# An encoder layer on one core: split first loads, squares and evictions, row tiles fetched three steps ahead, and a second output buffer for four compact tiles

## The chip, the core and the metric

The kernel is one program on one core of a Trainium2 chip. The metric is the device time of one execution in microseconds (us). The profile names the engines PE (TensorE, matmuls), PEld (its weight loads), DVE (VectorE), ACT (ScalarE), POOL (GpSimd) and SP (SyncE, which here only issues transfers). A matmul's result lies in one of the banks of the accumulator memory; a bank can be used again only after ACT and DVE have read it out, which is called evicting here.

## The reference

One layer of a bidirectional encoder is applied to two batches with the same weights: a prompt of 1024 rows and a sample of 512 rows, each row 1024 wide.

```python
h = rms_norm(x, pre_w)
cols = h @ w_in           # q|k, v, o, gates, z of branch A; q, k, v, z of branch B; merge gates
y_a = o * headnorm(mlstm_fwd + mlstm_bwd) * silu(z_a)       # 4 heads x 256, chunks of 128
y_b = mix(three dilated window attentions, 8 heads x 64) * silu(z_b)
merged = sigmoid(g_a) * (y_a @ w_proj_m) + sigmoid(g_b) * (y_b @ w_proj_a)
out = x + rms_norm(merged @ w_out, post_w)
```

All is in float32. The three attention groups have the windows and dilations (128, 1), (512, 4) and (2048, 16).

## The kernel before

**Products.** A float32 product is made of three matmuls on split operands: each operand is a high part (ACT's rounded copy) and a low part (DVE's difference), and `mm3` (L233 to L235) issues high x high, low x high, high x low. So every operand of a product, a weight or a row tile, passes ACT and DVE first: weights at L296 (ACT, `wh`) and L302 (DVE, `wl`).

**The beginning.** The first value columns are computed by a scheme of block combinations: `value_group` issues products of combined blocks named B11, B21 and so on. `lead` prepares B11: for each of the four row tiles of 128 rows it takes the sum of squares (`root`: ACT squares at L320, POOL makes the mean and the power -1/2 at L321 and L322), scales the identity by the result (L406, `u2b`), and PE turns and scales the row tile with it (L408) into four banks, k = 0 to 3, each 128 x 512. Then each bank is evicted as a high part (ACT, L412) and a low part (DVE, L413). PE's first value product (L233 to L235, tiles `d<-v,Hh`) reads them. Behind it stand the squares of the other four row tiles (ACT, L422), their scaling (DVE, L427), and the pieces of B21: for k = 0 to 3 `put` turns four row tiles on PE (L446), evicts the bank (ACT, L453), adds a matmul that takes the high part away (L459) and copies the low part (ACT, L460). `with_m1` sets where those pieces stand between the matmuls.

**The second half.** From 1720 us on, attention tiles of the branch B stand between the matmuls of the output branches. `branches` builds the work of one block of 512 rows: before a unit of projection, the rows of branch A's output, tiles of 128 x 512, are fetched from memory into three buffers in turn (`rows_in`: sraw, ymr0, ymr1) and split into high and low parts by `split`, ACT at L2121, DVE at L2122. `along` advances this generator once in three or four steps of the unit that runs. The fetches are issued on POOL's queue (L274), as are the weights w_out and w_pm (L285). An engine runs its instructions in the order in which they were written, so a wait at the head of its queue delays all behind it. `final` is the output product: two banks named `dense` are filled in turn, and each is evicted by ACT (L2231, the squares) and DVE (L2233, the product with the post weight) before PE may use it again.

**Compact attention tiles.** For the group with the largest dilation, `compact` computes four tiles at a time and gathers their output in a buffer `ot`: DVE copies the sums (L1707, `ot<-st`), ACT the output (L1708), and two stores (SP, L249) bring it to `og_b`. For the sample there is one such buffer for four tiles (`four`), so that L1707 of the next four must wait for both stores. `sg`, a tile of 512 columns, is used by the gates elsewhere.

Of the kernel before, what the change touches and what calls it, by code (L numbers as in the profile page):

```python
# [22 lines left out]
F32 = mybir.dt.float32  # L23
F32R = mybir.dt.float32r
AF = mybir.ActivationFunctionType
OP = mybir.AluOpType
# [3 lines left out]
P = 128  # L30
D = 1024
KT = D // P
BLK = 512
# [4 lines left out]
EPS = 1e-6  # L38
# [5 lines left out]
OW = 132  # L44
# [160 lines left out]
class Net:  # L205
# [111 lines left out]
    def root(self, xt, r, junk):  # L317
# [5 lines left out]
        return r[:, 2:3]  # L323

    def norm(self, xt, r, junk, pw=None):
# [64 lines left out]
    def combos(self, ps, H, xt, r, junk, pw, plus, minus, again, diag):  # L390
# [12 lines left out]
        def lead():  # L403
            ps_ = [ps.tile([P, BLK], F32, name="d") for _ in range(4)]
            for t in range(4):
                nc.vector.tensor_scalar(diag[t], self.ident, self.root(xt[0][t], r[t], junk), None, op0=OP.mult)  # L406
                for k in range(4):
                    nc.tensor.matmul(ps_[k][:, t * P:(t + 1) * P], a0[t][:, k * P:(k + 1) * P], diag[t], start=t == 0,  # L408
                                     stop=True, skip_group_check=True)
            for k in range(4):  # L410
                hi, lo, w = H[0][B11][:, k], H[1][B11][:, k], self.prew[:, k:k + 1]
                self.high = nc.scalar.activation(hi, ps_[k], AF.Copy, scale=w)  # L412
                self.low = nc.vector.scalar_tensor_tensor(lo, ps_[k], w, hi.bitcast(F32), op0=OP.mult, op1=OP.subtract)  # L413

        roots = {}

        def norm(i, t, j):

            if i and j and t % 2 == 0:
                two = r[4 + t // 2].rearrange("p (a b) -> p a b", a=3)  # L420
                for a in range(2):
                    nc.scalar.activation(junk, xt[i][t + a], AF.Square, accum_out=two[:, 0, a:a + 1])  # L422
                nc.gpsimd.tensor_scalar(two[:, 1], two[:, 0], 1.0 / D, EPS, op0=OP.mult, op1=OP.add)
                nc.gpsimd.tensor_tensor(two[:, 2], two[:, 1], self.mhalf, op=OP.pow)
                roots.update({t: two[:, 2, :1], t + 1: two[:, 2, 1:]})
            x, c = xt[i][t], slice(j * BLK, (j + 1) * BLK)
            return nc.vector.scalar_tensor_tensor(x[:, c], x[:, c], roots[t] if i else r[t][:, 2:3], pw[:, c], op0=OP.mult, op1=OP.mult)  # L427
# [165 lines left out]
    def value_group(self, T, H, us, co, ps, begin, wide):  # L593
# [27 lines left out]
        if True:  # L621
# [3 lines left out]
            def with_m1():  # L625
# [8 lines left out]
                low.append(split(wa[:, 1]))  # L634
                with self.tc.issue_after(last.ins), self.tc.issue_after(self.splits[1].ins):
# [7 lines left out]
                low.append(last.ins)  # L643
                rest = [put(B21, 0)]
                yield
                for k in range(1, 4):
                    rest.append(put(B21, k))
                    rest.pop(0)()
                rest.pop(0)()
                yield  # L650
# [1226 lines left out]
    def attend(self, T, fill, steps, first, banks, outs, after=None, beside=None, at=()):  # L1877
# [5 lines left out]
        with ExitStack() as st:  # L1883
# [18 lines left out]
            else:  # L1902
                o = sb.tile([P, outs * OW], F32, name="ot", bufs=1)
                self.ot = Rot(self, [o[:, i * OW:(i + 1) * OW] for i in range(outs)])
                four = Rot(self, [o[:, :4 * OW]])

# [191 lines left out]

    def split(self, T, b, row, places, halves):

# [9 lines left out]
        for j, (hi, lo) in enumerate(halves):  # L2110
            for k in range(6):
                if k < 4:
                    r = row + 4 * j + k
                    t = self.rows_in.pop(0)
                    self.rows_in.append(t)
                    got.append(t)
                    with self.tc.issue_after(self.loaded.ins):
                        self.fetch(("ym", T.S, min(r // 2, 4)), t[:, :w], T.ym[r, :, b * BLK:b * BLK + w], self.side)
                if k > 1:
                    t = got.pop(0)  # L2120
                    nc.scalar.activation(hi[:, k - 2, :w], t[:, :w], AF.Copy)  # L2121
                    nc.vector.tensor_sub(lo[:, k - 2, :w], t[:, :w], hi[:, k - 2, :w].bitcast(F32))  # L2122
                yield
# [20 lines left out]
    def branches(self, T, b, odd, before):  # L2144
# [28 lines left out]
        def proj_a(weights):  # L2173
            for ct in range(KT):
# [5 lines left out]
                for k in range(4):  # L2180
# [4 lines left out]
                    if k == 3:  # L2185
# [6 lines left out]

        return (self.along(before, lambda: self.split(T, b, 0, [(odd, 0, 1), (odd, 2, 1)], yb), 3)
                + self.along([Unit([(a["w_pm"][ct],) for ct in range(KT)], proj_m)],
                             lambda: self.split(T, b, 8, [(1 - odd, 1, 2)], ya), 4)
                + [Unit([(a["w_pa"][ct],) for ct in range(KT // 2)], proj_a)])
# [84 lines left out]
def body(tc, a):  # L2281
# [3 lines left out]
    with ExitStack() as st:  # L2285
# [12 lines left out]
        with ExitStack() as s1:  # L2298
# [4 lines left out]
            with ExitStack() as sv:  # L2303
# [21 lines left out]
                nc.scalar.dma_start(N.prew, a["prewc"])  # L2325
                for t in range(4):
                    rows(0, t)
                weights(0, 0)
                for t in range(4):
# [107 lines left out]
        with ExitStack() as s1:  # L2437
# [35 lines left out]
            with ExitStack() as s2:  # L2473
# [3 lines left out]
                nc.gpsimd.memset(N.sraw, 0.0)  # L2477
                N.sg = Rot(N, [sp.tile([P, BLK], F32R, name="sg")])
                ym = N.pool(s2, "ym", 1, "right")
# [105 lines left out]
```

## Time and profile before

| what | value |
|---|---|
| three runs | 2191.48, 2193.38, 2189.7 us; median 2191.48 |
| the profiled execution | 2191.66 us |
| its span in the trace | 2189.9 us |
| mean granted clock of PE | 1.0 |
| busy share | PE 99%, PEld 85%, DVE 67%, ACT 50%, POOL 32% |
| waits of PE that the list shows | 3.2 us before its first matmul, for a load; eight others, from 0.2 to 1.0 us, 3.8 us in all |

A row of the timeline gives start and duration in us, engine, line, operation, output and inputs; in brackets the idle time of the engine just before it and what ended that. Matmuls overlap: the start of one to the start of the next is the pace. In a row of a group, the last numbers are the busy time in us, the mean of one in ns, and the idle time before.

### The profile page before, as it was taken

What the parts mean: (1) busy time and instruction counts of PE and PEld (TensorE: products, weight loads), DVE (VectorE), ACT (ScalarE), POOL (GpSimd) and SP (SyncE); (2) the same over time, 40 slices, a digit from 0 to 9 for tenths busy, and PEclk for the clock granted to TensorE, in tenths of its full rate; (3) what the DMA queues carried; (4) which work ended last, traced back from release to release, by engine and by line L of the source; (5) the groups of instructions that cost most, each with busy time, mean ns of one, the idle gap of its engine ahead of it and who ended that gap; (6) DMA issues with size and microseconds to landing.
All of it is one profiled execution on the core that took longest, in us unless ns stands there. A gap on an engine that the chain in (4) does not pass through costs nothing.

```text
span 2189.9 us, 33604 instructions
## 1 busy us (share of the span) xinstructions
PE 2175.2 (99%) x11626; PEld 1857.3 (85%) x11626; DVE 1457.3 (67%) x2923; ACT 1085.2 (50%) x2227; POOL 702.2 (32%) x990
## 2 busy tenths in 40 slices
PE   9999999999999999999999999999999999999998
PEld 8988888888888888888888889998788888888887
DVE  7766564657778555547888765574668755656674
ACT  7322333344444333446777666666755544544332
POOL 1000332333333222326677650011045522232331
PEclk9999999999999999999999999999999999999999
DMA  3641454733333222367646558877768786776773
GB/s 138 190 141 67 151 162 144 229 108 116 112 110 116 78 77 97 135 227 250 218 158 219 183 172 255 236 237 202 200 234 275 242 295 198 227 244 200 239 241 106
DMA packets 205460, 395.62 MB, mean 181 GB/s; under 512 B 36361, under 2 KB 117961, under 8 KB 205290
## 3 DMA queue, kind: packets, MB, share of 16 engines
q1 hardware_dynamic: 174984, 281.39, 40.5%
q0 software_dynamic: 26704, 99.50, 14.2%
q10 hardware_dynamic: 3602, 12.59, 1.4%
q8 instruction: 92, 1.51, 0.3%
q14 instruction: 78, 0.64, 0.1%
HBM read 274.71 MB, written 118.69 MB: 180 GB/s over the span
## 4 chain that ended last, share of the span: by engine, by line
PE 92%; issue 1%; DMA 1%; DVE 1%; POOL 0%; ACT 0%; DVEq 0%; POOLq 0%
PE d L234 13%; PE d L233 13%; PE d L235 13%; PE dense L233 13%; PE dense L235 12%; PE dense L234 12%; PE lg L1771 2%; PE pt L1801 1%; PE o L1844 1%; PE num L233 1%; PE num L235 1%; PE num L234 1%; DMA sraw<-ym_a 1%; PE num L1467 1%; PE o L1823 1%
## 5 line engine op out<-in xcount | busy, mean ns | idle before, releaser
L233 PE MATMUL dense<-H,wh 128*128 128x512 f32 x664 | 269.5, 406 | 0.0
L234 PE MATMUL dense<-H,wh 128*128 128x512 f32 x664 | 260.4, 392 | 0.0
L235 PE MATMUL dense<-H,wl 128*128 128x512 f32 x664 | 260.4, 392 | 0.0
L233 PE MATMUL d<-Hh,phla 128*128 128x512 f32 x608 | 236.5, 389 | 0.0
L235 PE MATMUL d<-Hh,phla 128*128 128x512 f32 x608 | 236.5, 389 | 0.0
L234 PE MATMUL d<-Hl,phla 128*128 128x512 f32 x608 | 236.5, 389 | 0.0
L302 DVE TENSOR_TENSOR wl<-wraw,wh 128x1024 fp32r<-128x1024 f32 (+1 forms) x121 | 150.4, 1245 | 50.0 <-ACT wh L296 49.9
L235 PE MATMUL d<-Hh,phlb 128*128 128x512 f32 x456 | 177.4, 389 | 0.0
L233 PE MATMUL d<-Hh,phlb 128*128 128x512 f32 x456 | 177.4, 389 | 0.0
L234 PE MATMUL d<-Hl,phlb 128*128 128x512 f32 x456 | 177.4, 389 | 0.0
L296 ACT ACTIVATE wh<-wraw 128x1024 fp32r<-128x1024 f32 (+1 forms) x124 | 128.1, 1036 | 67.0 <-PE dense L234 20.7
L235 PEld LDWEIGHTS dense<-H,wl 128*128 128x128 f32 x664 | 124.7, 188 | 28.1
L764 POOL TENSOR_TENSOR psum_w<-pw_raw 128x512 f32<-128x512 f32 x38 | 55.4, 1458 | 276.7 <-DMA pw_raw<-w_in 206.9
L233 PEld LDWEIGHTS dense<-H,wh 128*128 128x128 f32 x664 | 125.1, 188 | 16.8 <-issue 1.2
L234 PEld LDWEIGHTS dense<-H,wh 128*128 128x128 f32 x664 | 125.3, 189 | 14.7
L1790 DVE CUSTOM_DVE_ANT_0 ls<-lg,bias 128x256 f32<-128x256 f32 (+2 forms) x240 | 78.8, 350 | 86.6 <-PE lg L1771 61.5
L234 PEld LDWEIGHTS d<-Hl,phla 128*128 128x128 f32 x608 | 114.1, 188 | 23.7
L233 PEld LDWEIGHTS d<-Hh,phla 128*128 128x128 f32 x608 | 114.1, 188 | 23.7
L235 PEld LDWEIGHTS d<-Hh,phla 128*128 128x128 f32 x608 | 114.1, 188 | 23.7
L782 POOL TENSOR_TENSOR psum_w<-pw_raw,psum_w 128x512 f32<-128x512 f32 x38 | 49.3, 1298 | 251.7 <-DVE phla L746 251.7
L1794 ACT ACTIVATE ls<-ls,nm 128x256 f32<-128x256 f32 (+1 forms) x192 | 87.3, 456 | 73.0 <-DVE nm L1792 48.0
L233 PE MATMUL d<-v,Hh 128*128 128x484 f32 (+1 forms) x336 | 121.3, 361 | 0.2
(657 smaller groups left out, 5834.5 us busy)
## 6 DMA issues: line engine op xcount, KB each, us to landing
pw_raw<-w_in SPq DMA_DIRECT2D x76, 512.0 KB, 4.1
wraw<-w_in SPq DMA_DIRECT2D x63, 512.0 KB, 4.4
aqk_a<-pwk SPq DMA_DIRECT2D x32, 512.0 KB, 6.9
wraw<-w_pm POOLq DMA_DIRECT2D x24, 512.0 KB, 6.0
wraw<-w_out POOLq DMA_DIRECT2D x24, 512.0 KB, 4.1
Q<-aqk_a SPq DMA_DIRECT2D x20, 512.0 KB, 6.2
wraw<-w_v POOLq DMA_DIRECT2D x22, 430.0 KB, 6.5
aqk_b<-sw SPq DMA_DIRECT2D x36, 256.0 KB, 6.7
```

Of the source, the lines that this page charges most:

```text
L233: nc.tensor.matmul(out, lh, rh, start=start, stop=False, **kw)
L234: nc.tensor.matmul(out, lh, rl, start=False, stop=False, **kw)
L235: nc.tensor.matmul(out, ll, rh, start=False, stop=stop, **kw)
L296: high = nc.scalar.activation(hi[:, :n], raw[:, :n], AF.Copy)
L302: low = (self.lows or nc.vector).tensor_sub(lo[:, :n], raw[:, :n], hi[:, :n].bitcast(F32))
L764: self.nc.gpsimd.tensor_add(s[:, 0], ws[1][:, 0], ws[1][:, 1])
L782: nc.gpsimd.tensor_sub(s[:, 1], wa[:, 1], s[:, 1])
L1467: nc.tensor.matmul(pn, hi[:, j], z[:, c1], start=j == 0 and z is v[0], stop=False)
L1771: nc.tensor.matmul(lg[:, hh], q[hh][:, qs], z.rearrange("p (n j) -> p n j", j=P)[:, pair], start=z is k[hh], stop=z is not k[hh])
L1790: nc.vector.tensor_tensor_reduce(out=ls[rows, hh], in0=ts["lg"][hh][rows, of], in1=bt[rows, hh, by], scale=1.0, scalar=NEG, op0=OP.add, op ...
L1794: self.held = self.held[-3:] + [nc.scalar.activation(ls[:, hh], ls[:, hh], AF.Exp, bias=nm[:, hh:hh + 1], accum_out=ot[:, 128 + hh:129 + hh])]
L1801: nc.tensor.transpose(pp[:, hh * nk + x], ts["ls"][:, hh, x * P:(x + 1) * P], self.ident)
```

## The change

Four edits. First, the loads and the first steps of the beginning: the fourth row tile and the first weight tile come as two transfers each; the fourth tile's square is made in two halves, DVE the first, ACT the second; the first of the four evictions is made in two halves of 256 columns; the squares of the other four tiles are written together; and the turned blocks of B21 for k = 0 and 1 both stand ahead of the second half of the value product. Second, `split` converts row k - `lead` before it fetches row k, with `lead` 3 instead of 2 (2 remains where more than one unit stands before the projection). Third, `four` turns between `ot` and the tile `sg`, which grows from 512 to 528 columns. Line numbers after the change are 11 to 23 higher (L412 is L429, L2121 is L2132, L2231 is L2249).

```diff
+    def root_of_halves(self, xt, r, junk):
+        nc = self.nc
+        a, b = (slice(i * BLK, (i + 1) * BLK) for i in range(2))
+        nc.vector.tensor_tensor_reduce(out=junk[:, a], in0=xt[:, a], in1=xt[:, a], scale=1.0 / D, scalar=EPS, op0=OP.mult, op1=OP.add,
+                                       accum_out=r[:, 0:1])
+        nc.scalar.activation(junk[:, b], xt[:, b], AF.Square, scale=D ** -0.5, accum_out=r[:, 3:4])
+        nc.vector.tensor_add(r[:, 1:2], r[:, 0:1], r[:, 3:4])
         nc.gpsimd.tensor_tensor(r[:, 2:3], r[:, 1:2], self.mhalf[:, :1], op=OP.pow)
         return r[:, 2:3]
...
-            for k in range(4):
-                hi, lo, w = H[0][B11][:, k], H[1][B11][:, k], self.prew[:, k:k + 1]
-                self.high = nc.scalar.activation(hi, ps_[k], AF.Copy, scale=w)
-                self.low = nc.vector.scalar_tensor_tensor(lo, ps_[k], w, hi.bitcast(F32), op0=OP.mult, op1=OP.subtract)
+            for k, a, b in ((0, 0, 2), (0, 2, 4), (1, 0, 4), (2, 0, 4), (3, 0, 4)):
+                hi, lo, p = (x[:, a * P:b * P] for x in (H[0][B11][:, k], H[1][B11][:, k], ps_[k]))
+                w = self.prew[:, k:k + 1]
+                with ExitStack() as st:
+                    if k + a:
+                        st.enter_context(self.tc.issue_after(self.high.ins))
+                        st.enter_context(self.tc.issue_after(self.low.ins))
+                    self.high = nc.scalar.activation(hi, p, AF.Copy, scale=w)
+                    self.low = nc.vector.scalar_tensor_tensor(lo, p, w, hi.bitcast(F32), op0=OP.mult, op1=OP.subtract)
...
-            if i and j and t % 2 == 0:
+            for b in (0, 2) if i and j and t == 0 else ():
...
-                rest = [put(B21, 0)]
+                rest = [put(B21, 0), put(B21, 1)]
                 yield
-                for k in range(1, 4):
+                for k in range(2, 4):
                     rest.append(put(B21, k))
                     rest.pop(0)()
-                rest.pop(0)()
+                rest.pop(0)(), rest.pop(0)()
...
-                four = Rot(self, [o[:, :4 * OW]])
+                four = Rot(self, [o[:, :4 * OW], self.late_ot])
...
-            for k in range(6):
+            for k in range(4 + lead):
+                if k >= lead:
+                    t, z = got.pop(0), k - lead
+                    nc.scalar.activation(hi[:, z, :w], t[:, :w], AF.Copy)
+                    nc.vector.tensor_sub(lo[:, z, :w], t[:, :w], hi[:, z, :w].bitcast(F32))
                 if k < 4:
...
-                if k > 1:
-                    t = got.pop(0)
-                    nc.scalar.activation(hi[:, k - 2, :w], t[:, :w], AF.Copy)
-                    nc.vector.tensor_sub(lo[:, k - 2, :w], t[:, :w], hi[:, k - 2, :w].bitcast(F32))
...
+        return (self.along(before, lambda: self.split(T, b, 0, [(odd, 0, 1), (odd, 2, 1)], yb, 2 if len(before) > 1 else 3), 3)
...
+                for i in range(2):
+                    nc.sync.dma_start(xt[0][3][:, i * BLK:(i + 1) * BLK], A.x[3 * P:4 * P, i * BLK:(i + 1) * BLK])
+                for i in range(2):
+                    c = slice(i * 2 * VW, (i + 1) * 2 * VW)
+                    nc.sync.dma_start(begin[1][:, 0, c], a["w_vp"][0, 0][:, c])
...
+                sg = sp.tile([P, 4 * OW], F32R, name="sg")
+                N.sg, N.late_ot = Rot(N, [sg[:, :BLK]]), sg.bitcast(F32)
```

ACT's order at the beginning, from the first eviction on. Before:

```order
L412 ACTIVATE Hh_96<-d,prew 128x512 x4
L422 ACTIVATE Hl_108,xr_124<-x_134 128x1024
L422 ACTIVATE Hl_108,xr_124<-x_135 128x1024
L422 ACTIVATE Hl_108,xr_125<-x_136 128x1024
L422 ACTIVATE Hl_108,xr_125<-x_137 128x1024
L479 ACTIVATE v_116<-v_118 128x1288
L453 ACTIVATE Hh_98<-d 128x512
L687 ACTIVATE u_161<-d 128x322
L453 ACTIVATE Hh_98<-d 128x512
L460 ACTIVATE Hl_105<-d 128x512
L453 ACTIVATE Hh_98<-d 128x512
L460 ACTIVATE Hl_105<-d 128x512
```

And after the change (L429 is the eviction, L470 the high part and L477 the low part of B21):

```order
L429 ACTIVATE Hh_96<-d,prew 128x256 x2
L429 ACTIVATE Hh_96<-d,prew 128x512 x3
L439 ACTIVATE Hl_108,xr_124<-x_134 128x1024
L439 ACTIVATE Hl_108,xr_124<-x_135 128x1024
L439 ACTIVATE Hl_108,xr_125<-x_136 128x1024
L439 ACTIVATE Hl_108,xr_125<-x_137 128x1024
L496 ACTIVATE v_116<-v_118 128x1288
L470 ACTIVATE Hh_98<-d 128x512 x2
L705 ACTIVATE u_163<-d 128x322
L470 ACTIVATE Hh_98<-d 128x512
L477 ACTIVATE Hl_105<-d 128x512
L470 ACTIVATE Hh_98<-d 128x512
```

The first eviction is two instructions, and the high parts of k = 0 and 1 stand next to each other; the fourth high part has one low part ahead of it where two stood before.

ACT's order in the output product of the prompt, around the second and third eviction L2231. Before:

```order
L2121 ACTIVATE H_18677<-ymr_17486 128x512
L1794 ACTIVATE ls,ot<-ls,nm 128x128 x2
L2121 ACTIVATE H_18677<-sraw 128x512
L1825 ACTIVATE ot<-o 128x128
L2231 ACTIVATE sw_7260,ss<-dense 128x512
L1794 ACTIVATE ls,ot<-ls,nm 128x128 x2
```

After, first the same place (L2249 is the eviction), then where the row's conversion L2132 now stands:

```order
L2132 ACTIVATE H_18682<-ymr_17491 128x512
L1812 ACTIVATE ls,ot<-ls,nm 128x128 x2
L1843 ACTIVATE ot<-o 128x128
L2249 ACTIVATE sw_7265,ss<-dense 128x512
L1812 ACTIVATE ls,ot<-ls,nm 128x128 x2
```

```order
L296 ACTIVATE Q_17486<-wraw_7147 128x1024
L2132 ACTIVATE H_18682<-sraw 128x512
L2249 ACTIVATE sw_7267,ss<-dense 128x512
L296 ACTIVATE wh_7150<-wraw_7146 128x1024
L1843 ACTIVATE ot<-o 128x128
L1823 ACTIVATE pts<-pt 128x256
L2132 ACTIVATE H_18682<-ymr_17490 128x512
```

The conversion of sraw has moved from ahead of the second eviction to ahead of the fourth, and the last row's (ymr) from there to behind the copies that follow.

POOL's queue at the same rows, before and then after:

```order
L274 DMA ymr_17485<-ym_a 128x512
L274 DMA ymr_17486<-ym_a 128x512
L274 DMA sraw<-ym_a 128x512
L285 DMA wraw_7142<-w_out 128x1024
L274 DMA ymr_17485<-ym_a 128x512
L285 DMA wraw_7141<-w_pm 128x1024
```

```order
L274 DMA ymr_17490<-ym_a 128x512
L274 DMA ymr_17491<-ym_a 128x512
L285 DMA wraw_7147<-w_out 128x1024
L274 DMA sraw<-ym_a 128x512
L285 DMA wraw_7146<-w_pm 128x1024
L274 DMA ymr_17490<-ym_a 128x512
```

Each of the last two rows is now fetched behind a weight tile that stood behind it before.

More of the change, by code (lines that the diff above doesn't have):

```diff
@@ L323, in root @@
         return r[:, 2:3]
+    def root_of_halves(self, xt, r, junk):
[5 more added lines that the diff above has]
+        nc.vector.tensor_add(r[:, 1:2], r[:, 0:1], r[:, 3:4])
+        nc.gpsimd.tensor_tensor(r[:, 2:3], r[:, 1:2], self.mhalf[:, :1], op=OP.pow)
+        return r[:, 2:3]
     def norm(self, xt, r, junk, pw=None):
@@ L405, in lead @@
             for t in range(4):
-                nc.vector.tensor_scalar(diag[t], self.ident, self.root(xt[0][t], r[t], junk), None, op0=OP.mult)
+                nc.vector.tensor_scalar(diag[t], self.ident, (self.root_of_halves if t == 3 else self.root)(xt[0][t], r[t], junk), None,
+                                        op0=OP.mult)
                 for k in range(4):
@@ L633, in with_m1 @@
                         last = norm(1, t, 1)
-                low.append(split(wa[:, 1]))
+                with self.tc.issue_after(self.squared.ins):
+                    low.append(split(wa[:, 1]))
                 with self.tc.issue_after(last.ins), self.tc.issue_after(self.splits[1].ins):
@@ L2097, in place, with split @@
         return self.take((("V0b", "V1b", "K0", "K1"), ("H0", "H1", "H2", "H3"))[which][i], dt).rearrange("p (k t) -> p k t", k=4)
-    def split(self, T, b, row, places, halves):
+    def split(self, T, b, row, places, halves, lead):
         nc = self.nc
@@ L2191, in proj_a @@
                     yield
-        return (self.along(before, lambda: self.split(T, b, 0, [(odd, 0, 1), (odd, 2, 1)], yb), 3)
+        return (self.along(before, lambda: self.split(T, b, 0, [(odd, 0, 1), (odd, 2, 1)], yb, 2 if len(before) > 1 else 3), 3)
                 + self.along([Unit([(a["w_pm"][ct],) for ct in range(KT)], proj_m)],
-                             lambda: self.split(T, b, 8, [(1 - odd, 1, 2)], ya), 4)
+                             lambda: self.split(T, b, 8, [(1 - odd, 1, 2)], ya, 3), 4)
                 + [Unit([(a["w_pa"][ct],) for ct in range(KT // 2)], proj_a)])
@@ L2325, in body @@
                 nc.scalar.dma_start(N.prew, a["prewc"])
-                for t in range(4):
+                for t in range(3):
                     rows(0, t)
-                weights(0, 0)
+                for i in range(2):
[3 more added lines that the diff above has]
+                    nc.sync.dma_start(begin[1][:, 0, c], a["w_vp"][0, 0][:, c])
                 for t in range(4):
@@ L2477, in body @@
                 nc.gpsimd.memset(N.sraw, 0.0)
-                N.sg = Rot(N, [sp.tile([P, BLK], F32R, name="sg")])
+                sg = sp.tile([P, 4 * OW], F32R, name="sg")
+                N.sg, N.late_ot = Rot(N, [sg[:, :BLK]]), sg.bitcast(F32)
                 ym = N.pool(s2, "ym", 1, "right")
```

6 lines of the change are left out of this document (3 added, 3 removed).

## The prediction

> **What bounds the kernel now.** I read the page's busy times first, then the list of waits by engine, then the timeline around each wait. Line numbers are those of the kernel before.
>
> ```profile
> span 2189.9 us, 33604 instructions
> ...
> PE 2175.2 (99%) x11626; PEld 1857.3 (85%) x11626; DVE 1457.3 (67%) x2923; ACT 1085.2 (50%) x2227; POOL 702.2 (32%) x990
> ...
> PE dense L233 <- DVE sw L2233: 1.0, 1, 1.0
> PE dense L235 <- DVE H L2190: 0.7, 1, 0.7
> ...
> PE d L235 <- DVE Hl L455: 0.4, 1, 0.4
> ```
>
> TensorE (PE) works in 2175.2 of 2189.9 us, so 14.7 us is all that any rearrangement can win without removing matmuls, and the change removes none. The waits list shows where PE stands for another engine: the two largest stalls behind the start, and the third row for a stall at 50 us that a rival below needs. Each is one stall (the middle number is the count). So the question is narrow: which stalls go, and what new ones come.
>
> A measurement of this kernel can tell about 0.2% from no change, that is 4.4 us.
>
> **The beginning.** The timeline, in order of time:
>
> ```profile
> 10.31 2.06 PE L408 MATMUL d<-u2b,v 128*128 128x128 f32 x17
> 10.67 0.29 DVE L406 TENSOR_SCALAR u2b<-ident,xr 128x128 f32<-128x128 f32 x1 [0.99 <-POOL xr L322]
> 11.74 2.42 ACT L412 ACTIVATE Hh<-d,prew 128x512 fp32r<-128x512 f32 x4 [0.27 <-PE d L408]
> 12.46 0.75 DVE L413 SCALAR_TENSOR_TENSOR Hl<-d,prew,Hh 128x512 fp32r<-128x512 f32 x1 [0.75 <-ACT Hh L412]
> 12.48 0.42 PE L233 MATMUL d<-v,Hh 128*128 128x322 f32 x1
> 13.26 0.42 PE L235 MATMUL d<-v,Hl 128*128 128x322 f32 x1 [0.22 <-DVE Hl L413]
> ...
> 20.96 0.48 PE L459 MATMUL d<-Hh,Hl 128*128 128x512 f32 x1
> 21.24 0.60 ACT L453 ACTIVATE Hh<-d 128x512 fp32r<-128x512 f32 x1 [0.51 <-PE d L446]
> 21.89 0.50 PE L459 MATMUL d<-Hh,Hl 128*128 128x512 f32 x1
> 22.21 0.61 ACT L453 ACTIVATE Hh<-d 128x512 fp32r<-128x512 f32 x1
> 22.87 0.50 PE L459 MATMUL d<-Hh,Hl 128*128 128x512 f32 x1
> 23.84 0.50 PE L459 MATMUL d<-Hh,Hl 128*128 128x512 f32 x1 [0.47 <-ACT Hh L453]
> ```
>
> *Split loads and the split square* (fourth row tile). The last diagonal u2b is done at 10.67 + 0.29 = 10.96 while PE is streaming its L408 matmuls from 10.31 without a gap, the last tile's standing at the end. Having that diagonal earlier moves nothing: cost and gain zero. The cover is about half a microsecond of earlier tiles' matmuls; the new DVE square has no row here, and it would have to be later than the 10.67 of today's diagonal by that much to show. The bytes on SP's queue keep their order.
>
> *Split first eviction.* PE starts L233 when ACT has converted a whole bank (0.69 us, 11.74 to 12.43, just before DVE's start) and L235 when DVE has the low part (12.46 to 13.21). In halves of 256 columns the nearest rows are other operations that read 256 columns from the accumulator:
>
> ```profile
> L1271 ACT ACTIVATE X<-num,r 128x256 f32<-128x256 f32 x32 | 14.9, 464 | 13.1 <-DVE r L1268 12.9
> L1273 DVE SCALAR_TENSOR_TENSOR X<-num,r,X 128x256 f32<-128x256 f32 x32 | 15.4, 483 | 0.9
> ```
>
> ACT's half: 0.69 - 0.46 = 0.23 us saved; DVE's half: 0.75 - 0.48 = 0.27 us. PE's L235 comes 0.5 us earlier, near 12.77. [...]
>
> What is late next: the new order makes ACT's second half wait for DVE's first half. ACT starts it at about 11.74 + 0.46 + 0.48 + two handovers of 0.03 = 12.74 and the second eviction some 0.34 later, at 13.08, where it was at 11.74 + 0.58 = 12.32 (four in 2.42, so (2.42 - 0.69) / 3 apart). So ACT's whole queue behind it (the squares L422 among them) is 0.76 us late, and DVE's with it. ACT is then what PE waits for, at the last L459 (23.84). Ahead of its fourth L453, the change lets transposes L446 of block k = 1 stand in PE's queue before the value product, so that ACT's 0.51 us of waiting at 21.24 goes, and one L460 moves behind it: half of 22.21 - 21.24, 0.48. Together 0.76 - 0.51 - 0.48 = -0.23: PE is 0.2 us early after 23.84, out of 0.5 that it had. The ends are 0 (halves at the price of wholes eat it) and -0.5 (ACT never late). I take **-0.25 us**, by the chain.
>
> **Rows three steps ahead.** The timeline where PE stands longest:
>
> ```profile
> 1903.49 0.55 POOL L274 DMA_DIRECT2D sraw<-ym_a  x1 [2.83 <-DVE H L2122]
> 1907.00 0.29 PE L235 MATMUL lg<-V0a,Q 128*128 128x256 f32 x1
> 1909.17 0.63 ACT L2121 ACTIVATE H<-sraw 128x512 fp32r<-128x512 f32 x1 [3.95 <-DMA sraw<-ym_a]
> 1909.86 0.59 ACT L2231 ACTIVATE sw<-dense 128x512 f32<-128x512 f32 x1
> 1910.35 0.39 PE L234 MATMUL dense<-Q,K 128*128 128x512 f32 x1
> 1910.58 0.39 PE L235 MATMUL dense<-Q,K 128*128 128x512 f32 x1
> 1911.26 0.68 DVE L2233 TENSOR_TENSOR sw<-dense,postw 128x512 f32<-128x512 f32 x1
> 1912.00 0.50 PE L233 MATMUL dense<-wh,V0b 128*128 128x512 f32 x1 [1.04 <-DVE sw L2233]
> ```
>
> The row tile sraw is fetched at 1903.49 and lands at 1909.17. ACT waits 3.95 us for it at the head of its queue, with the eviction L2231 behind; DVE's L2233 ends at 1911.94, and PE, which steps at 0.23 us (1910.35 to 1910.58), gets the bank 1910.58 + 0.23 to 1912.00, **1.19 us** late. After the change this conversion has gone behind that eviction, to where the next row (H<-ymr, 1922.76) stood. ACT was free 3.95 us before 1909.17, at 1905.2, so L2231 is done by 1906. On DVE short softmax pieces stand ahead of L2233; PE writes their input lg by 1907.3, and they took no more than 1911.26 - 1909.80 (the end of ACT's conversion) = 1.46 us, so L2233 ends near 1909.4, 1.4 us before PE asks. The stall goes: -1.19.
>
> What waits for the row now is the next eviction:
>
> ```profile
> 1918.09 0.55 POOL L274 DMA_DIRECT2D ymr<-ym_a  x1
> 1922.76 0.62 ACT L2121 ACTIVATE H<-ymr 128x512 fp32r<-128x512 f32 x1
> 1924.63 0.68 DVE L2233 TENSOR_TENSOR sw<-dense,postw 128x512 f32<-128x512 f32 x1
> 1926.22 0.40 PE L233 MATMUL dense<-wh,V0b 128*128 128x512 f32 x1
> DMA to landing us min/median/max: 2.7/5.3/8.3
> ymr<-ym_a POOLq DMA_DIRECT2D x1, 256.0 KB, 4.3
> ```
>
> On POOL's queue the sraw fetch now comes behind the weight load w_out, which POOL issues only when DVE frees its buffer, and takes the place of the ymr fetch of 1918.09. That one landed in 4.3 us, before 1922.76 (the last row, of this place), where all rows of this tile name need 2.7 to 8.3 us (the row above it). At 4.3 us nothing waits; L2233 ends at 1925.31 and PE asks for that bank at 1926.22, 0.9 us later. The last row's fetch goes behind the next weight load, w_pm; its conversion now stands after the softmax copies, and no eviction is right behind it. I take 0, with +2.7 us as the other end (8.3 us, less 1922.76 + 0.9 - 1918.09). The other splits of rows get the same order and have no wait of PE behind them in the list: 0 there too, with the same other end, which is a rival below.
>
> **A second buffer for four compact tiles.**
>
> ```profile
> 2022.19 1.17 SPq L249 DMA_DIRECT2D og_b<-ot  x2
> 2026.42 1.04 ACT L296 ACTIVATE wh<-wraw 128x1024 fp32r<-128x1024 f32 x1
> 2029.64 0.18 DVE L1707 COPY ot<-st 128x16 f32<-128x16 f32 x1 [2.90 <-ACT V0b L2121]
> 2031.72 0.39 PE L234 MATMUL dense<-wl,H 128*128 128x512 f32 x1
> 2032.09 0.69 DVE L2190 TENSOR_TENSOR H<-mg,H 128x512 fp32r<-128x512 f32 x1
> 2032.83 0.50 PE L235 MATMUL dense<-wh,H 128*128 128x512 f32 x1 [0.72 <-DVE H L2190]
> ```
>
> DVE stands 2.90 us before the small copy L1707 into ot. The engine named had long finished; what L1707 must wait for is the two stores of ot issued at 2022.19, since there is one buffer for four tiles. Behind it on DVE are L302, two L2122 and the L2190 that PE needs: PE is 2032.83 - 2031.72 - 0.23 = **0.88 us** late. With the copy going to sg, whose last store is long past, DVE is held by ACT's wh alone, to 2027.46: the copy's successors come 2029.64 + 0.1 - 2027.5 = 2.2 us earlier, and L2190 ends near 2030.5 (2032.78 before), 1.4 us before PE asks (2031.95). The stall goes: -0.88. No instruction is added; the ends are -0.88 and 0.
>
> **The sum** against the profiled execution: its time is 2191.66 us, the span 2189.9 and 1.76 around it; the median of the runs is 2191.48, 0.18 lower. -0.25 - 1.19 - 0.88 = -2.32: 2189.34 us for the profiled one, **2189.1 us** for a median, 0.11% less.
>
> **Rivals.**
>
> *The beginning gives all it has* (faster). The four L459 stand 0.93, 0.98 and 0.97 us apart. PE steps at 0.23 us for 512 columns; an L459 and four transposes of 128 columns would need 0.46 by that pace, and the last, without transposes ahead of it, 0.23: at most 0.47 + 0.52 + 0.74 = 1.73 us of waits. If ACT is not late they go, with the 0.5 at the eviction and the 0.4 at 50 us behind them: -2.63, with the two later stalls -4.7, 2186.8 us. For it: ACT had idle time in this stretch. Against: its queue is ready last at 23.84, and it is now later. Chance 0.24.
>
> *Late rows* (slower). Rows fetched behind a weight load, with the evictions behind their conversion on ACT, land late in the places where PE has two banks. It decides at 1922.76 + 0.9 - 1918.09 = 5.6 us from issue to landing; the median of 5.3 lies close below. At the longest, 8.3, a place costs 8.3 - 5.6 = 2.7 us. Were three of the six splits so, +8.1 - 2.3 = +5.8: 2197.3 us. Against: the very fetch of 1918.09 took 4.3, and one bad place alone leaves a time below today's or at it. Chance 0.12.
>
> *It does not do what it says* (no change). There are three row buffers, and three steps ahead a step must convert before it fetches, so a row may be waited for as before: the 1.19 stays, 2190.3 us. Against: the order shows the conversion behind the eviction. Chance 0.06. The forecast keeps 0.58.
>
> **Numbers.** The likeliest case gives 2189.1. Low end: the first rival, 2186.8, and 0.3 for it coming in a low run: 2186.5. High end: the stall that stays, 2190.3, with the 1.9 us by which the highest run lies over the median: 2192.2. What lies outside is the slower rival and the edges, under 2 in 10. Faster by over 0.2% (below 2187.1) needs the first rival nearly whole, about two thirds of its 0.24: with the forecast in very low runs, 0.17. Slower by over 0.2% (above 2195.9): most of the second rival, 0.10. The rest, 0.73, is within 0.2%.
>
> **What would show it.** Right: the rows for L2233 and L2190 gone from PE's waits, L2231 near 1905 in the timeline, the copy L1707 (into sg) with no wait, PE's first L235 near 12.8 and its fourth L459 near 23.6. Wrong: PE idle against the conversion of rows or an eviction behind it, a DMA wait of ACT over 1 us at the new places, or DVE starting its low halves so late that L235 waits at the second and third row tile of the first product.

## The result and the profile after

The changed kernel takes 2189.48 us (median of 22 runs, 2187.49 to 2191.32) where the kernel before, beside it on the same chip, takes 2192.17 (22 runs, 2189.7 to 2196.8): 2.69 us less, ratio 0.9986, interval 0.998 to 0.9992. The forecast was 2189.1. The gain is small, 0.12%, but the interval lies wholly below one: 22 runs of each tell some 1.3 us apart, finer than the 4.4 us that the forecast reckoned with. The profiled execution is 2189.48 us, its span 2187.7, against 2191.66 and 2189.9.

The waits list of the changed kernel, PE's rows (total, count, longest in us):

```profile
PE d L2358 <- DMA Hh<-prew: 2.3, 1, 2.3
PE d L420 <- DVE u2b L417: 1.1, 1, 1.1
PE num L1485 <- ACT X L1495: 0.6, 1, 0.6
PE tp L2049 <- DVE Q L2044: 0.5, 1, 0.5
PE sc L235 <- DVE kl L1416: 0.5, 1, 0.5
PE d L476 <- ACT Hh L470: 0.5, 1, 0.5
PE d L235 <- DVE Hl L472: 0.4, 1, 0.4
```

The two rows that led the list, for L2233 and L2190, are gone. What is left behind the start is no longer than 0.6 us. (The second row is not new work: here the first load came 1 us earlier, and PE waits behind it for the first diagonal instead.)

The timeline of the changed kernel at the first of the two stalls:

```profile
1907.82 0.39 PE L235 MATMUL dense<-wh,K 128*128 128x512 f32 x1
1908.25 0.60 ACT L2249 ACTIVATE sw<-dense 128x512 f32<-128x512 f32 x1 [1.06 <-PE dense L235]
1908.97 0.69 DVE L2251 TENSOR_TENSOR sw<-dense,postw 128x512 f32<-128x512 f32 x1 [0.72 <-ACT sw L2249]
1910.59 0.39 PE L235 MATMUL dense<-Q,K 128*128 128x512 f32 x1
1910.81 0.39 PE L233 MATMUL dense<-wh,V0b 128*128 128x512 f32 x1
```

ACT starts the eviction when PE has finished the bank; no row tile stands ahead of it. DVE ends at 1909.66, and PE steps from 1910.59 to 1910.81, its full pace, where it had waited from 1910.81 to 1912.00. Further down, the row that was moved:

```profile
1916.78 0.55 POOL L274 DMA_DIRECT2D sraw<-ym_a  x1
1921.10 0.62 ACT L2132 ACTIVATE H<-sraw 128x512 fp32r<-128x512 f32 x1
1921.62 0.57 ACT L2249 ACTIVATE sw<-dense 128x512 f32<-128x512 f32 x1
1922.97 0.68 DVE L2251 TENSOR_TENSOR sw<-dense,postw 128x512 f32<-128x512 f32 x1
```

It is converted 4.3 us after its issue, with no wait in brackets, and the eviction follows at once. The second stall:

```profile
2025.06 0.17 DVE L1725 COPY sg<-st 128x16 f32<-128x16 f32 x1
2025.89 1.23 DVE L302 TENSOR_TENSOR wl<-wraw,wh 128x1024 fp32r<-128x1024 f32 x1 [0.67 <-ACT wh L296]
2028.24 0.68 DVE L2208 TENSOR_TENSOR H<-mg,H 128x512 fp32r<-128x512 f32 x1
```

The small copy into sg waits for nothing (2.90 us before), and ACT's weight copy is what DVE waits for next. The beginning:

```profile
8.47 0.69 DVE L329 CUSTOM_DVE_ANT_0 Hl<-v 128x512 fp32r<-128x512 f32 x1
8.53 0.69 POOL L321 TENSOR_SCALAR xr<-xr 128x1 f32<-128x1 f32 x1 [0.45 <-ACT Hl L320]
10.90 0.29 DVE L417 TENSOR_SCALAR u2b<-ident,xr 128x128 f32<-128x128 f32 x1 [0.66 <-POOL xr L333]
11.71 1.28 PE L420 MATMUL d<-u2b,v 128*128 128x128 f32 x10
12.36 0.47 ACT L429 ACTIVATE Hh<-d,prew 128x256 fp32r<-128x256 f32 x1 [1.25 <-DMA x<-x_prompt]
12.86 0.48 DVE L430 SCALAR_TENSOR_TENSOR Hl<-d,prew,Hh 128x256 fp32r<-128x256 f32 x1 [0.93 <-ACT Hh L429]
13.38 2.21 ACT L429 ACTIVATE Hh<-d,prew 128x256 fp32r<-128x256 f32 x4 [0.55 <-DVE Hl L430]
13.40 0.41 PE L235 MATMUL d<-v,Hl 128*128 128x322 f32 x1
24.16 0.50 PE L476 MATMUL d<-Hh,Hl 128*128 128x512 f32 x1 [0.48 <-ACT Hh L470]
51.15 0.41 PE L235 MATMUL d<-v,Hl 128*128 128x322 f32 x1 [0.41 <-DVE Hl L472]
```

PE's first L235 stands at 13.40 and the fourth L476 at 24.16, both later than the forecast's 12.8 and 23.6, and even than before (13.26 and 23.84). The reason lies ahead of them. In the kernel before, the same two ends are:

```profile
11.65 0.72 PE L408 MATMUL d<-u2b,v 128*128 128x128 f32 x5
50.82 0.41 PE L235 MATMUL d<-v,Hl 128*128 128x322 f32 x1 [0.41 <-DVE Hl L455]
```

The last scaling matmul ends at 11.65 + 0.72 = 12.37 before and at 11.71 + 1.28 = 12.99 after, for a reason that the change has no part in (PE's pace, last section). From that end to the stall at 50 us, which both kernels have, it is 38.45 us before and 38.16 after. I call this stretch the distance; it measures the beginning apart from the pace. It hardly varies: in the four executions with the old beginning, here and below, it is 38.45 to 38.48, and in the five with the new one and no further edit of its evictions 38.14 to 38.16, whatever the pace was. So the beginning gains 0.29 us, and this pair of profiles hides it behind 0.62 us of slower matmuls.

### The profile page after: what moved, and what is told of

The parts are those of the page before. It is cut to its first block, busy times and chain, and to the rows that moved or that the text cites. A ratio compares the mean times of both kernels' runs of the same rounds, so it can differ in the third digit from the quotient of the medians.

```text
span 2187.7 us, 33607 instructions
## 1 busy us (share of the span) xinstructions
PE 2174.0 (99%) x11626; PEld 1857.4 (85%) x11626; DVE 1455.5 (67%) x2927; ACT 1086.1 (50%) x2228; POOL 704.6 (32%) x989
## 4 chain that ended last, share of the span: by engine, by line
PE 91%; DMA 3%; DVE 2%; issue 2%; POOL 1%; ACT 1%; SPq 0%; DVEq 0%; POOLq 0%; ACTq 0%
PE d L233 14%; PE d L235 14%; PE d L234 14%; PE dense L233 11%; PE dense L234 11%; PE dense L235 11%; PE lg L1789 2%; PE pt L1819 1%; DMA wraw<-w_pm 1%; PE o L1862 1%; PE num L233 1%; PE num L234 1%; PE num L235 1%; PE a L1192 1%; PE o L1841 1%
## 5 line engine op out<-in xcount | busy, mean ns | idle before, releaser
L235 PE MATMUL dense<-H,wl 128*128 128x512 f32 x664 | 260.3, 392 | 0.0
L235 PE MATMUL d<-Hh,phla 128*128 128x512 f32 x608 | 236.5, 389 | 0.0
L235 PE MATMUL d<-Hh,phlb 128*128 128x512 f32 x456 | 177.4, 389 | 0.0
L235 PEld LDWEIGHTS dense<-H,wl 128*128 128x128 f32 x664 | 124.7, 188 | 28.0
L235 PEld LDWEIGHTS d<-Hh,phla 128*128 128x128 f32 x608 | 114.1, 188 | 23.8
```

The costliest lines, as they stand in the source:

```text
L235: nc.tensor.matmul(out, ll, rh, start=False, stop=stop, **kw)
```

## The experiments

### The parts alone

The kernel before with only the beginning; with only the rows three steps ahead; with only the second buffer; and with the last two:

```diff
-            for k in range(6):
+            for k in range(4 + lead):
+                if k >= lead:
...
-                four = Rot(self, [o[:, :4 * OW]])
+                four = Rot(self, [o[:, :4 * OW], self.late_ot])
```

Expected of the beginning alone:

> Only the beginning's edits (split loads, split square, split first eviction, the turned blocks put forward). Theory A (by the prediction's steps): -0.25 us against the kernel before, between -0.5 and 0, the two late stalls (1.2 us at the output product, 0.9 us at the compact tiles) stay in the trace. Theory B (the beginning now costs time, because the profiled execution after the change left the beginning 0.3 us later than before): +0.3 us or more. Theory C (the measured 2.7 us hold more than the two stalls): -0.6 us or more.

Of the rows alone:

> Only the rows three steps ahead. Theory A: -1.2 us; PE's wait for the eviction near 1910 us is gone from the list, the one near 2032 us stays. Rival (late rows): a new wait of PE of 1 us or more behind an eviction or a row conversion, and a time that is not lower than before.

Of the second buffer alone:

> Only the second buffer for four compact tiles. Theory A: -0.9 us; PE's wait near 2032 us is gone, the one near 1910 us stays. Rival (DVE is held by ACT's conversions or by the weights there anyway): the copy no longer waits but PE does, the time within 0.3 us of before.

Of rows and buffer:

> Rows and second buffer together, the beginning as before. Theory A: the two stalls add, -2.1 us; the full change is 0.25 us lower than this. Theory B: this is as fast as the full change or faster (-2.4 to -2.7 us). Theory C: the full change is at least 0.6 us lower than this.

Measured, each against a kernel before at 2192.25 us:

| kernel | median us | ratio, interval | PE late at 1910 / at 2031, us |
|---|---|---|---|
| beginning alone | 2191.96 | 0.9999 [0.9990, 1.0007] | 0.9 / 0.5 |
| rows alone | 2191.81 | 0.9997 [0.9989, 1.0006] | none / 0.3 |
| buffer alone | 2191.35 | 0.9994 [0.9985, 1.0002] | 0.4 / none |
| rows and buffer | 2189.76 | 0.9991 [0.9982, 1.0000] | none / none |

The intervals are nearly 4 us wide, so single parts cannot be told apart by time: the forecasts for the parts lie inside them, but so do most of their rivals. The traces can tell them apart: each edit removes its own stall and no other. By the medians, beginning alone (-0.3) and rows with buffer (-2.5) add to -2.8, about the whole. The last column holds the surprise: a stall that stays is not 1.19 or 0.88 us again. The row tile at 1910 in the kernel with the beginning alone, then in that with the buffer alone:

```profile
1909.62 0.63 ACT L2139 ACTIVATE H<-sraw 128x512 fp32r<-128x512 f32 x1 [3.31 <-DMA sraw<-ym_a]
```

```profile
1908.96 0.63 ACT L2121 ACTIVATE H<-sraw 128x512 fp32r<-128x512 f32 x1 [2.67 <-DMA sraw<-ym_a]
```

ACT waits 3.95, 3.31 or 2.67 us for the same transfer in three executions, and PE is late by 1.2, 0.9 or 0.4. A stall behind a transfer has a spread of its own; one profile gives one draw of it. My -1.19 and -0.88 were the largest of the three draws that I have of each.

The kernel with the beginning alone also shows what the small copy waits for, where the list of the kernel before named an engine that had long finished: the store of `ot`.

```profile
2029.55 0.17 DVE L1725 COPY ot<-st 128x16 f32<-128x16 f32 x1 [2.54 <-DMA og_b<-ot]
```

### The eviction: one piece, two pieces, two banks

Whole: the changed kernel with the first eviction in one piece. Two banks: its halves lie in two banks, so that the first needs only the first two row tiles:

```diff
-            for k, a, b in ((0, 0, 2), (0, 2, 4), (1, 0, 4), (2, 0, 4), (3, 0, 4)):
+            for k, a, b in ((0, 0, 4), (1, 0, 4), (2, 0, 4), (3, 0, 4)):
```

```diff
+            bank = lambda k, t: ps_[4 if k == 0 and t > 1 else k]
...
-                    if k + a:
+                    if k:
```

Expected of the whole eviction:

> The full change with the first eviction in one piece, as before the change; the turned blocks of B21 stay put forward. By the prediction's chain ACT's queue is then early by 0.51 + 0.48 us against before, PE restarts 0.5 us later at L235 but no longer waits for ACT behind the transposes: 0.3 to 0.6 us less from the last L420 to the product behind B21 than with the halves, that is, the split eviction costs more than it gains. Rival (the split is worth its 0.5 us): that distance is 0.3 us longer or more than in the full change (11.89 us there).

Of two banks:

> The full change with the two halves of the first eviction in two banks, so that ACT's second half does not wait for DVE's first, and the first half needs only the first two row tiles. Theory (the chain of the two engines through one bank put ACT's queue 0.76 us back, and ACT is what PE waits for at the fourth L476): ACT's squares and the fourth high part of B21 come 0.7 us earlier, PE's wait there (0.48 us) shrinks to below 0.2, and after the last L420 PE reaches the next product 0.3 to 0.8 us sooner than in the full change; time 0.3 to 0.8 us lower. Rival (DVE's scaling or the norms bind there): the wait of PE stays within 0.1 us of 0.48.

Whole: 2189.17 us (ratio 0.9988 [0.9979, 0.9997]). Its timeline:

```profile
11.67 0.94 PE L420 MATMUL d<-u2b,v 128*128 128x128 f32 x7
21.92 0.60 ACT L470 ACTIVATE Hh<-d 128x512 fp32r<-128x512 f32 x1 [0.46 <-PE d L463]
50.54 0.41 PE L235 MATMUL d<-v,Hl 128*128 128x322 f32 x1 [0.41 <-DVE Hl L472]
```

The distance is 50.54 - 12.61 = 37.93, shorter than the 38.16 with the split. So the split eviction, which looks like the heart of the beginning, costs 0.23 us; the rest of the beginning gives 38.45 - 37.93 = 0.52 (probably the new order of squares and turned blocks, which were not tried apart). The sign is as expected, the size is below the 0.3 to 0.6: without the split ACT begins its squares 0.8 us earlier, counted from the last scaling matmul, but then waits 0.46 us at the third high part for PE's turned block, which the expectation did not count.

Two banks: **2186.93 us** (2185.53 to 2188.03, ratio 0.9978 [0.997, 0.9987]), the lowest median of this study. Its timeline:

```profile
9.65 0.48 ACT L430 ACTIVATE Hh<-d,prew 128x256 fp32r<-128x256 f32 x1 [0.27 <-PE d L421]
10.20 0.48 DVE L431 SCALAR_TENSOR_TENSOR Hl<-d,prew,Hh 128x256 fp32r<-128x256 f32 x1
12.17 0.94 PE L421 MATMUL d<-u2b,v 128*128 128x128 f32 x7
13.24 0.31 PE L235 MATMUL d<-v,Hl 128*128 128x322 f32 x1
50.23 0.41 PE L235 MATMUL d<-v,Hl 128*128 128x322 f32 x1 [0.41 <-DVE Hl L473]
```

The first half is high and low by 10.7, while PE still scales the other two tiles; L235 starts 0.13 us behind the last scaling matmul (0.41 in the changed kernel, 0.89 before), ACT's second half waits for no one, and the distance is 50.23 - 13.11 = 37.12: 1.04 us less than the change as made. The medians differ by 2.55, but the intervals of the two ratios overlap; 1.04 is what the trace shows.

This is more than the expected 0.3 to 0.8, and one step of that theory fails: PE's wait for the fourth high part did not shrink below 0.2, it is 0.47 us still, which was the sign of its rival. That wait does not tell how late ACT is. ACT starts its fourth high part 0.95 us after its third in this kernel, in the changed one and in the kernel before (22.21 to 23.16 there), with one low part between them, and PE is ready for it each time; what moves is when both start.

### The square

The changed kernel with the fourth square in one piece, and the same with two banks:

```diff
-                nc.vector.tensor_scalar(diag[t], self.ident, (self.root_of_halves if t == 3 else self.root)(xt[0][t], r[t], junk), None,
+                nc.vector.tensor_scalar(diag[t], self.ident, self.root(xt[0][t], r[t], junk), None,
```

> The changed kernel with the fourth tile's square in one piece again (ACT alone). In the changed kernel POOL's small step L321 of the third tile took 0.69 us instead of 0.19 while DVE's half square ran, and the last diagonal came at 10.90 us instead of 10.67. Theory 1 (the split square costs nothing and gains nothing, since PE reaches the last tile only near 11.9): POOL's step is 0.19 again, the last diagonal starts near 10.7, the distance from PE's last scaling step to the product behind B21 stays 11.89 +- 0.02, and the time 2189.5 within 0.5 us. Rival (the earlier square matters): the last scaling step comes 0.2 us or more later than the clock alone explains, and the time is 0.2 to 0.5 us above the changed kernel.

With two banks:

> The changed kernel with the halves of the first eviction in two banks, and the fourth square in one piece. Theory 1: as with the two banks alone, distance from the last scaling step to the stall near 50 us 36.8 us, time 2186.9 within 0.5. Rival (the split square matters once the eviction is no longer late): 0.2 to 0.5 us above 2186.9.

Measured: 2189.71 us (0.9986 [0.9977, 0.9995]) and 2187.51 (0.9979 [0.9971, 0.9988]): no difference in time from the kernels with the split square. But neither theory saw why the first of them has its last scaling step late, the sign of its rival:

```profile
10.63 0.83 DVE L497 TENSOR_TENSOR v<-v,v 128x644 fp32r<-128x644 f32 x1 [0.94 <-ACT v L496]
11.31 1.55 POOL L497 TENSOR_TENSOR v<-v,v 128x644 fp32r<-128x644 f32 x1 [0.43 <-ACT v L496]
11.38 1.56 DVE L417 TENSOR_SCALAR u2b<-ident,xr 128x128 f32<-128x128 f32 x1
12.99 1.16 PE L420 MATMUL d<-u2b,v 128*128 128x128 f32 x8 [1.53 <-DVE u2b L417]
```

The first half of the first weight tile, which the split loads bring early, now stands on DVE ahead of the last diagonal; the diagonal then takes 1.56 us instead of 0.29 beside POOL's half of the same work, and PE waits 1.53. Its scaling ends at 14.15, 1.16 us later than in the profile of the changed kernel. The median does not show that loss (2189.71 against 2189.48, with some 2 us of uncertainty each): in this execution PE's pace rose near 10.2, so that the wait is bare. Had it stayed slow, the 24 instructions of the first three tiles would have ended, by estimate, at 6.99 + 0.38 (the first step) + 23 x 0.213 = 12.3 and PE had waited 0.7; that this evens out the median is argued, not shown. In the profile of the kernel with two banks the diagonal stays ahead, and PE does not wait for it.

### Rows made late

The changed kernel with three transfers of 256 KB each put on POOL's queue ahead of the fetches that moved, in both blocks (their data are not used):

```diff
+                    for x in range(3 if row == 0 and lead == 3 and j and k > 1 else 0):
+                        with self.tc.issue_after(self.loaded.ins):
+                            self.side.dma_start(self.junk[b, r, x], T.ym[(r + 1 + x) % 8, :, b * BLK:(b + 1) * BLK])
```

> The full change, with three more transfers of 256 KB from memory to memory on POOL's queue ahead of each of the two moved row fetches of a block (the third and fourth row of the second half, in both blocks that fetch three ahead); their result is not used. Prices the slower rival of the prediction: the row lands 2 to 4 us later than the 4.3 us of before. By its working (it decides at 5.6 us from issue to landing, every further microsecond stops PE as long) PE waits 1 to 2.5 us for the fourth eviction near 1925 us and the time is 1 to 5 us above the full change. Rival (there is more cover than worked out): no wait of PE above 0.3 us there, time within 1 us of the full change.

Measured: 2193.27 us, ratio 1.0008 [0.9999, 1.0018], whose interval does not meet that of the changed kernel (0.998 to 0.9992): 3.8 us dearer. Its waits of PE, then rows of ACT at the output product and of DVE in the second block:

```profile
PE tp L2049 <- DVE cw L2021: 1.9, 1, 1.9
PE tp L2049 <- DVE Q L2044: 1.6, 1, 1.6
PE dense L233 <- ACT K L2132: 0.6, 1, 0.6
```

```profile
1808.22 0.63 ACT L2132 ACTIVATE K<-ymr 128x512 fp32r<-128x512 f32 x1 [1.64 <-DMA ymr<-ym_a]
1921.32 0.60 ACT L2252 ACTIVATE sw<-dense 128x512 f32<-128x512 f32 x1
1923.92 0.63 ACT L2132 ACTIVATE H<-sraw 128x512 fp32r<-128x512 f32 x1 [0.51 <-DMA sraw<-ym_a]
2092.83 0.17 DVE L2022 TENSOR_TENSOR cw<-cw,V1a 128x8 f32<-128x8 f32 x1 [1.98 <-DMA V1a<-og_b]
2101.89 0.68 DVE L2044 TENSOR_TENSOR Q<-Q 128x512 f32<-128x512 f32 x1
```

The time is as expected, its way is not, and the rival itself was not put to the test. At the prompt's output product PE does not wait, because ACT's order is another one in this kernel: the eviction (L2252, 1921.32) now stands ahead of the row's conversion (1923.92), which comes 2.8 us later than in the changed kernel (1921.10) and holds up no eviction. So the 5.6 us from which a late row should stop PE remain untried. The third row is a row tile converted late, at 1808 us and 0.6 us dear, but not by this edit: the first of the added transfers is issued at 1916.81. In the changed kernel ACT waits 1.53 us for the same tile there, and PE, which gets there later, loses 0.3. Most of the cost falls in the second block, where POOL's queue also brings V1a and the other inputs of branch B's merge: DVE waits 1.98 us for V1a (0.57 in the changed kernel), its L2044 ends late, and PE waits at the merge's transposes L2049 1.9 + 1.6 us against 0.5. The orders of ACT, DVE and POOL there changed too, so the run prices the added transfers with all that they reorder, not the late row.

### PE's pace

The beginning with extra work for PE ahead: nine matmuls on one row; eight of the identity by itself (128 rows), on top of two banks and a whole square; and four.

```diff
+                for _ in range(3):
+                    nc.tensor.matmul(hot[:, :P], one, one, start=True, stop=True)
...
+                    for _ in range(6 if i else 0):
+                        nc.tensor.matmul(hot[:, :P], one, one, start=True, stop=True)
```

```diff
+                hot = ps.tile([P, BLK], F32, name="d")
+                for _ in range(8):
+                    nc.tensor.matmul(hot[:, :P], N.ident, N.ident, start=True, stop=True)
```

Of the nine:

> The full change, with nine extra one-row matmuls of 128 columns on PE ahead of the first scaling matmuls (three before and six behind the two that spread the norm weights), whose result nothing uses. In the traces so far PE's scaling matmuls (L420, before L408) step at 0.42 us up to some point between 9.8 and 12 us and at 0.22 us after it, and the point differs from execution to execution of the same beginning. Theory (PE starts slow and speeds up after some time of work): with PE busy from the start, the steps are 0.22 us from the first row tile on, the last L420 is bound by its diagonal near 11 us and ends near 12, L233 starts near 12.2 in place of 12.9 to 13.7, and the time is 0.7 to 1.5 us below the full change. Rival (the slow steps come from something else, such as the loads): the steps stay at 0.42 us to 10 us or later, time as the full change or up to 0.5 us above.

Of the eight:

> As the kernel with two banks and a whole square, but PE first multiplies the identity by itself eight times (128 rows, float32, results unused), before the two one-row products of the norm weight. Theory A (PE steps at half pace until it has had about 3 us of work on 128 rows): the eight steps take 0.43 us each from about 1.5 us on, the one-row products follow, the scaling matmuls step at 0.22 us from their first, the last one is bounded by the last diagonal (near 10.7 + 0.29 us) and starts near 11.6 instead of 12.7: time about 2185.8, 1.1 us below the kernel without the eight. Theory B (the moment of the faster pace does not depend on the work that PE had): slow steps until 10 to 13 us as in all runs so far, time 2186.9 within 0.5, or up to 1 us above it where the norm weight comes later.

Of the four:

> The same with four such products instead of eight (1.7 us of work at 0.43 us each). Theory A: not enough by itself, the faster pace comes between 7 and 12 us, the time lies between those of the kernels with none and with eight, 2185.8 to 2186.9. Theory B: slow until 10 to 13 us, 2186.9 within 0.5.

Measured: 2191.04 us (0.9995 [0.9986, 1.0004]), 2190.18 (0.9988 [0.998, 0.9997]) and 2188.02 (0.998 [0.9971, 0.9989]): none is faster than its own base (2189.48, 2187.51, 2187.51). The times alone do not decide, since all three have a wait of PE of 0.8 us at L348, near 957 us, that no other kernel here has; the extra products take one of the banks named `d`, and I suppose that those after it turn differently. So I go by the start. With the nine, PE reaches the scaling matmuls at 9.51 us instead of 7.09, and they are slow until 12.87: the expected 0.22 from the first on does not come. With the four they are slow until 11.84, which both of its theories allow. A view of stretches of time, with PE's busy time and instruction count first and the granted clock in the column PEclk (third from the end), of the kernel before and of that with eight:

```profile
7.30:9.30 2.00, 2.00 (x10) 2.00 (x11) 0.67 (x2) 1.87 (x3) 1.37 (x4) 1.00 1.04 428
10.30:12.00 1.70, 1.70 (x18) 1.70 (x17) 1.03 (x2) 1.43 (x3) 0.79 (x2) 1.00 1.03 417
```

```profile
1.60:4.80 3.20, 3.20 (x15) 3.20 (x16) 0.00 (x0) 1.85 (x4) 0.00 (x0) 1.00 0.93 281
12.00:14.00 2.00, 2.00 (x12) 2.00 (x11) 1.29 (x2) 0.00 (x0) 0.82 (x1) 1.00 1.03 414
14.30:14.90 0.60, 0.60 (x8) 0.60 (x7) 0.00 (x0) 0.28 (x1) 0.00 (x0) 1.00 1.04 416
```

Before, ten matmuls take 2 us at first and eighteen take 1.7 us later: the pace doubles, though the column says 1.00 in both. With eight ahead, 3.5 us of the same kind of work from 1.48 us on buys nothing: the scaling matmuls start at 8.90, behind the slow one-row ones, and are slow until about 14.2. The last of them ends at 15.25, against 12.93 without the eight. (The last diagonal too was late there, as with the whole square, but PE reached its tile only near 14.2.) So the theory that 3 us of full matmuls at any earlier time would do falls, and so does the other, that the moment is fixed near 10 to 13 us.

## Why the prediction was right

**The beginning, -0.25.** Measured -0.29 by the distance. The chain held step by step: ACT's squares 0.81 us late, counted from the last scaling matmul (forecast 0.76), halves of 0.47 and 0.48 us (forecast 0.46 and 0.48), L235 0.48 us nearer to the scaling (0.89 to 0.41; forecast 0.5), ACT's second half waiting 0.55 us for DVE's first, and the fourth high part still what PE waits for, 0.30 us earlier by the same clock (23.84 - 12.37 = 11.47, now 24.16 - 12.99 = 11.17; forecast 0.2). The split as made costs 0.23 us against the whole eviction. What the trace shows as the price is the 0.55 us that ACT's second half waits in the shared bank; the same halves in two banks, as many instructions, gain 37.93 - 37.12 = 0.81 against the whole. For the length of a half the rows of other operations with 256 columns were right to 0.01 us.

**The split square, zero.** The time agrees, but two of its steps fail. The last diagonal came later (10.90, not 10.67): while DVE's half square ran, POOL's small step for the third tile took 0.69 us instead of 0.19. And the cover of half a microsecond holds only while DVE's queue has nothing ahead of the diagonal; I did not look at what the early weight half would do there, which the whole square then showed at 1.53 us of PE's time.

**Rows three ahead, -1.19.** The stall is gone, but the bank was not ready by 1906: PE itself finished it at 1908.2. ACT being free is not enough; the bank must be full. The margin was 1.15 us where I had 1.4, so the sign stood. The row landed within 4.3 us, below the 5.6 from which it would have cost. The size was one draw: 1.2, 0.9 or 0.4 us.

**Second buffer, -0.88.** Gone as said, with ACT's weight copy next; here too the size is one draw, 0.9, 0.5 or 0.3.

**The sum, -2.32.** Measured -2.69 in the medians (by the interval, 1.8 to 4.4) and -2.18 in the profiled pair, which is +0.62 of pace, -0.29, -1.20, -0.88 and a remainder of -0.43. The remainder lies in small steps elsewhere: the same matmul of PE just before the first stall (L235 on Q and K) starts at 1910.58 us before and at 1910.59 after, so the +0.33 with which the changed kernel left the beginning was made up by then. That the forecast lies 0.4 from the median is partly luck: two terms were large draws. The three draws of each average 0.8 and 0.6; with the 0.29 that is 1.7, just below the interval, and where the rest of the measured gain comes from is not shown.

**The rivals.** "The beginning gives all it has" failed: PE still waits for the fourth high part (0.48 us) and at 50 us (0.41), as its counterpart said. "Late rows" did not come about: at the places whose order changed, ACT waits at most 0.7 us for a row; what a late one would cost there is not measured. "It does not do what it says" is out by the order and the trace.

## What to carry to other kernels

Here a split eviction paid only where its first half could start before the rest was written (0.81 us gained in two banks, 0.23 lost in one): give the halves banks of their own, or leave the instruction whole. A stall behind a transfer is a spread, not a number (here PE was 1.2, 0.9 or 0.4 us late behind the same transfer): look at the same wait in several executions before it becomes a term. When a load comes earlier, look at where the work that it frees is put on every engine, above all ahead of an instruction that the first chain needs (PE waited 1.53 us for such an instruction here). And when an experiment adds work to a queue, compare the order of every engine first: the rows made late changed the very order that they were to test.

## What the runs showed of the hardware

**PE's pace at the start.** In all fourteen profiled executions PE's first scaling matmuls step at 0.213 us an instruction and later at 0.11. The change comes 2.9 to 5.7 us after the first of them (10.05 us in the kernel before, 11.3 in the changed, 12.8 with the rows alone), and differs from execution to execution of the same beginning, by 2.8 us from the earliest to the latest. Eight earlier matmuls, followed by one-row ones, did not shorten it: from 1.48 us on they ran, and the scaling was slow from 8.90 until about 14.2. What does count remains open.

**DVE and POOL.** A POOL step of 0.19 us took 0.69 beside DVE's square, and a DVE step of 0.29 us took 1.56 beside POOL's 1.55 (1.57 beside 1.56 in the kernel with the eight products), each pair ending within 0.1 us.
